# A Griffin-style encoder block: gates and branches by seven products, two of the weights' sums by accumulating DMAs

## The chip, the core and the metric

The kernel runs on one core of a Trainium2 chip. The engines of the core are named as the profile names them: PE (TensorE, matmuls), DVE (VectorE), ACT (ScalarE), POOL (GpSimd) and SP (SyncE, which here only issues DMAs). Each engine works through its own queue in order. The metric is the device time in microseconds of one execution; shorter is better. The kernel before takes 2479.7 us (median of 3 runs, 2479.21 to 2479.93).

## The reference

One layer over 512 tokens with 2048 features, all in float32:

```
h  = RMSNorm(x)
[q|k|v|u|ga|gb] = h @ W_in              # 3*1024 + 1024 + 2048 + 2048 columns
yA = attention(q, k, v)                 # 16 heads, 64-token chunks, 9-chunk band, relative bias
yB = pooling mixer(u)                   # trailing means over 2/4/8/16 tokens, per-group 256x256 map, scale
m  = sigmoid(ga) * (yA @ P_A) + sigmoid(gb) * (yB @ P_B)      # P_A, P_B: 1024 x 2048
x  = x + m @ W_o                        # 2048 x 2048
x  = x + (silu(g) * up) @ W_down        # [g|up] = RMSNorm(x) @ W_gate_up, 2048 x 11264; W_down 5632 x 2048
out = RMSNorm(x)
```

## The kernel before

**Precision.** Every float32 operand of a matmul is split into a rounded part (hi) and a rest (lo) in the float32r format, and every product is three matmuls into one PSUM bank: `product` (L210) and lines 925 to 927. A matmul has a 128x128 stationary operand and a 128x512 moving one. Weights arrive by SP's DMA queue in tiles of 128x1024 (512 KB); ACT copies such a tile to hi, DVE subtracts to get lo.

**First part, panels.** `panel` (L215) computes 256 output columns of h @ W for all 512 tokens, with the weights stationary and the turned x (XH, XL) moving. The order is q, k, v in four groups (with attention of the group's heads interleaved as generators), four panels of u (each followed by the generator `pooling`), and then the gates and branches: for yB the list `b_order` alternates panels of gate b and of P_B, for yA the list `a_order` does so with gate a and P_A. A gate panel is 16 x 2 x 3 = 96 matmuls and a branch panel 8 x 2 x 3 = 48; there are 8 of each for a and for b, so 16 x 96 + 16 x 48 = 2304 matmuls. The evacuations `evac_gate`, `evac_b` and `evac_a` multiply, add and store the merged m by features in DRAM (`m_dram`). At the end four P_A panels stand in a row (`N_TAIL`), and beside them `build_merged` builds the first forms for W_o.

**Second part, jobs.** `run_job` (L906) computes a block of 1024 inner rows by 1024 columns for all 512 tokens by a Strassen-like scheme with seven products P1, P5, P6, P3, P7, P2, P4 instead of eight block products; a product is 24 matmuls (two units of 12), a job 14 units and 168 matmuls where the direct way has 192. Here the activations are stationary, as seven prepared *forms* (`build_forms`, L721: for each of two halves seven hi by ACT, seven lo and four sums by DVE, each 128x512), and weights move. The seven weight operands come from four quarters of the weights, which are kept in tiles r11, r12, r21, r22 per unit: DVE adds r11 += r12 (for P5, L851), r11 += r22 (P6, L853), r12 += r22 (P7, L855) and r21 += r11 (P4, L857). `t_to`, `hi2_to` and `lo2_to` issue sum, hi and lo of a unit four, three and three units ahead of its matmuls, `load2_to` its load 7 units ahead.

The products of a job gather in PSUM in X (P1, P6, P7, P4) and Y (P5, P3; then a new Y for P2), and `evacuate` (L878) takes them out one unit after a product's end: as c tiles of a ring of six, which accumulate across products, and across jobs by accumulating DMAs of POOL's queue (`c += gp` and the like). What is done with a finished block is the job's `done`: storing partial results, squares, SiLU and product (`hidden`), turning by PE transposes (128x128) for the next forms. Such work is written as generators in the list `active`; `step()` runs each one's next stretch once per unit, so it fixes between which units of PE an instruction stands. There are 4 jobs for W_o (called o), 22 for W_gate_up (g; eleven for each half of the inner dimension), 12 for W_down (d; two with half the length): 36 x 168 + 2 x 84 = 6216 matmuls. Forms lie in two pools, A and B, used in turn.

**The end.** `last_done` and `store` (L1075, L1093) take the last d job's blocks through the final norm; `store(0)` for the first 256 tokens starts after block 11, `store(1)` after block 21.

Of the kernel before, what the change touches and what calls it, by code (L numbers as in the profile page):

```python
# [16 lines left out]
P = 128  # L17
# [15 lines left out]
PRODUCTS = ("P1", "P5", "P6", "P3", "P7", "P2", "P4")  # L33
# [13 lines left out]
def hybrid_block_kernel(  # L47
# [211 lines left out]
    for i in range(PWID // CU):  # L259
        add_panel(w_in, KD, 3 * AW + i * CU)  # L260
    GA, GB = 3 * AW + PWID, 3 * AW + PWID + D
    n_blk = D // CU
    b_order = [("g", 0), ("g", 1)] + [x for i in range(n_blk) for x in ((("y", i), ("g", i + 2)))]
    b_order = [x for x in b_order if x[1] < n_blk]
    for what, i in b_order:
        if what == "g":
            add_panel(w_in, KD, GB + i * CU)
        else:
            add_panel(w_branch_b, KB, i * CU)
    a_order = [x for i in range(n_blk - N_TAIL) for x in (("g", i), ("y", i))]  # L270
    a_order += [(what, i) for what in "gy" for i in range(n_blk - N_TAIL, n_blk)]
    for what, i in a_order:
        if what == "g":
            add_panel(w_in, KD, GA + i * CU)
        else:
            add_panel(w_branch_a, KA, i * CU)
# [100 lines left out]
    Q, K, KL, VS, YA = {}, {}, {}, {}, {}  # L377
    LOHALF, HIHALF = slice(0, DH), slice(DH, 2 * DH)
# [70 lines left out]
    def attention(h):  # L449
# [110 lines left out]
        nc.vector.tensor_tensor(YA[pair][hi_half], o_ps[LOHALF], low[LOHALF], op=ALU.add)  # L560

# [47 lines left out]
    YBH, YBL = {}, {}  # L609

    def pooling(g):
# [24 lines left out]
        for e in range(2):  # L636
# [6 lines left out]
            YBH[m], YBL[m] = split(ps, "yb", gains[:, 2 * KD + m:2 * KD + m + 1], mid)  # L643
            yield

    for i in range(PWID // CU):
        panel(KD, XH, XL, lambda oc, ps, i=i: evac_u(2 * i + oc, ps))
        active.append(pooling(i))


    SG, T = {}, {}
    m_dram = {}

    def evac_gate(m, ps):
        SG[m] = slot(F32, "sg")
        nc.vector.tensor_tensor(SG[m], ps, r_bc, op=ALU.mult)
        nc.scalar.activation(SG[m], SG[m], AF.Sigmoid)

    def evac_b(m, ps):
        T[m] = SG.pop(m)  # L660
        nc.vector.tensor_tensor(T[m], ps, T[m], op=ALU.mult)

    def evac_a(m, ps):
        s = SG.pop(m)
        nc.vector.tensor_tensor(s, ps, s, op=ALU.mult)
        nc.vector.tensor_tensor(s, T.pop(m), s, op=ALU.add)
        m_dram[m] = tc.dram_tile([P, 512], F32, name=f"m_dram{m}")
        nc.gpsimd.dma_start(m_dram[m], s)

    for what, i in b_order:  # L670
        if what == "g":
            panel(KD, XH, XL, lambda oc, ps, i=i: evac_gate(2 * i + oc, ps))
            if i == 1:
                drain()
        else:
            panel(KB, YBH, YBL, lambda oc, ps, i=i: evac_b(2 * i + oc, ps))
    YAH, YAL = {}, {}

# [547 lines left out]
```

## Time and profile before

| | |
|---|---|
| median of 3 runs | 2479.7 us |
| profiled execution: its own time / its span | 2477.76 us / 2476.0 us |
| PE busy / DVE busy / ACT busy / POOL busy | 2414.8 / 1734.9 / 1158.7 / 129.8 us |
| panels of q, k, v, u with attention | 0 to 422 us |
| gates and branches | 422 to 965 us |
| jobs o / g and d | 965 to 1129 us / 1129 to 2457 us |
| end (final norm, stores) | 2457 to 2476 us |
| moved by DMA | 352.19 MB, mean 142 GB/s |

The profile is of one execution. Its span runs from the first to the last instruction; the execution's own time is 1.8 us longer. PE is the engine that is busy nearly all of the time, so a microsecond in which PE has nothing to do is lost, and a matmul that falls away is gained, as long as nothing else takes its place. Stretches are given in us from the span's start.

### The profile page before, as it was taken

How to read it: one execution, taken by the hardware profiler on the slowest of the kernel's cores; microseconds unless marked ns; L12 is line 12 of the kernel's file. 1: busy time of each engine (PE TensorE's matmuls, PEld its weight loads, DVE VectorE, ACT ScalarE, POOL GpSimd, SP SyncE). 2: the span in 40 equal slices, each digit the busy share in tenths (PEclk: the TensorE clock that was granted, in tenths of full speed). 3: DMA queues.
4: the chain of work that ended last, by engine and by line, in shares of the span. 5: the costliest groups of instructions: out<-in, count | busy, mean ns of one | idle time of the engine just before them, and what ended most of it. 6: DMA issues, size and time to landing. Idle time of an engine off the chain costs nothing.

```text
span 2476.0 us, 28917 instructions
## 1 busy us (share of the span) xinstructions
PE 2414.8 (98%) x11221; PEld 2002.4 (81%) x11221; DVE 1734.9 (70%) x2026; ACT 1158.7 (47%) x1484; POOL 129.8 (5%) x226
## 2 busy tenths in 40 slices
PE   9999999999999999999999999989999999999996
PEld 7899888888888887787788888867788787887785
DVE  6556656523343338989787787888888888798977
ACT  5445443322222224467544544555645555555645
POOL 0000000000000001110000000001010000000010
PEclk9999999999999999999999999999999999999998
DMA  5322232233333335765354453657365555464564
GB/s 180 98 90 90 83 108 83 90 96 100 95 109 107 111 117 193 219 189 212 112 204 142 165 202 119 198 146 186 102 187 137 171 151 171 126 194 135 158 188 127
DMA packets 203145, 352.19 MB, mean 142 GB/s; under 512 B 11304, under 2 KB 95856, under 8 KB 202880
## 3 DMA queue, kind: packets, MB, share of 16 engines
q1 hardware_dynamic: 177616, 263.50, 31.0%
q0 software_dynamic: 24096, 84.49, 14.6%
q10 hardware_dynamic: 1296, 2.36, 0.2%
q8 instruction: 88, 1.44, 0.2%
q14 instruction: 49, 0.40, 0.0%
HBM read 289.44 MB, written 60.86 MB: 141 GB/s over the span
## 4 chain that ended last, share of the span: by engine, by line
PE 82%; DVE 11%; issue 3%; ACT 2%; DMA 0%; ACTq 0%; SPq 0%; DVEq 0%
PE psd L211 10%; PE psd L213 10%; PE psd L212 10%; PE psx L925 8%; PE psx L927 8%; PE psx L926 8%; PE psy L925 7%; PE psy L926 6%; PE psy L927 6%; DVE low L873 4%; DVE c L890 1%; ACT hiw L865 1%; PE psd L424 1%; PE psd L425 1%; PE psd L426 1%
## 5 line engine op out<-in xcount | busy, mean ns | idle before, releaser
L865 ACT ACTIVATE hiw<-r 128x1024 fp32r<-128x1024 f32 x518 | 546.8, 1059 | 556.6 <-PE psx L927 241.7
L873 DVE TENSOR_TENSOR low<-r,hiw 128x1024 fp32r<-128x1024 f32 x518 | 631.7, 1221 | 225.1 <-ACT hiw L865 224.5
L925 PE MATMUL psx<-low,fP 128*128 128x512 f32 x1184 | 467.0, 394 | 14.7 <-DVE c L890 7.3
L927 PE MATMUL psx<-hiw,fP 128*128 128x512 f32 x1184 | 462.3, 390 | 0.0
L926 PE MATMUL psx<-hiw,fP 128*128 128x512 f32 x1184 | 461.9, 390 | 0.0
L168 DVE TENSOR_TENSOR lo<-raw,hi 128x1024 fp32r<-128x1024 f32 (+1 forms) x161 | 195.8, 1218 | 309.4 <-ACT hi L159 309.2
L925 PE MATMUL psy<-low,fP 128*128 128x512 f32 x888 | 350.5, 395 | 23.3 <-DVE low L873 21.3
L159 ACT ACTIVATE hi<-raw 128x1024 fp32r<-128x1024 f32 (+1 forms) x161 | 169.2, 1053 | 416.5 <-PE psd L213 299.2
L927 PE MATMUL psy<-hiw,fP 128*128 128x512 f32 x888 | 346.1, 390 | 0.0
L926 PE MATMUL psy<-hiw,fP 128*128 128x512 f32 x888 | 345.8, 389 | 0.0
L211 PE MATMUL psd<-xh,lo 128*128 128x512 f32 x864 | 338.5, 392 | 0.0
L213 PE MATMUL psd<-xl,hi 128*128 128x512 f32 x864 | 336.8, 390 | 0.0
L212 PE MATMUL psd<-xh,hi 128*128 128x512 f32 x864 | 336.7, 390 | 0.0
L925 PEld LDWEIGHTS psx<-low,fP 128*128 128x128 f32 x1184 | 222.8, 188 | 67.9 <-DVE c L890 11.3
L927 PEld LDWEIGHTS psx<-hiw,fP 128*128 128x128 f32 x1184 | 222.8, 188 | 47.4
L926 PEld LDWEIGHTS psx<-hiw,fP 128*128 128x128 f32 x1184 | 223.0, 188 | 44.9
L925 PEld LDWEIGHTS psy<-low,fP 128*128 128x128 f32 x888 | 166.7, 188 | 65.6 <-DVE low L873 29.2
L927 PEld LDWEIGHTS psy<-hiw,fP 128*128 128x128 f32 x888 | 166.6, 188 | 35.5
L926 PEld LDWEIGHTS psy<-hiw,fP 128*128 128x128 f32 x888 | 166.8, 188 | 33.4
L213 PEld LDWEIGHTS psd<-xl,hi 128*128 128x128 f32 x864 | 162.2, 188 | 34.2
L212 PEld LDWEIGHTS psd<-xh,hi 128*128 128x128 f32 x864 | 162.4, 188 | 32.1
L211 PEld LDWEIGHTS psd<-xh,lo 128*128 128x128 f32 x864 | 162.3, 188 | 32.1
(205 smaller groups left out, 2789.5 us busy)
## 6 DMA issues: line engine op xcount, KB each, us to landing
r<-in_w_gate_up SPq DMA_DIRECT2D x176, 512.0 KB, 8.2
raw<-in_w_in SPq DMA_DIRECT2D x127, 512.0 KB, 3.6
r<-in_w_down SPq DMA_DIRECT2D x88, 512.0 KB, 7.7
x1d<-c POOLq DMA_DIRECT2D x48, 512.0 KB, 7.9
gp<-c POOLq DMA_DIRECT2D x44, 512.0 KB, 5.5
c<-gp POOLq DMA_DIRECT2D x33, 512.0 KB, 5.2
r<-in_w_out SPq DMA_DIRECT2D x32, 512.0 KB, 8.1
raw<-in_w_branch_b SPq DMA_DIRECT2D x16, 512.0 KB, 3.3
```

What stands on the lines that cost most here:

```text
L159: nc.scalar.activation(hi_t[i][:, :m], raw_t[i][:, :m], AF.Copy)
L168: nc.vector.tensor_tensor(lo_t[i][:, :m], raw_t[i][:, :m], hi_t[i].bitcast(F32)[:, :m], op=ALU.subtract)
L211: mm(ps, wl, ah, start=start, stop=False)
L212: mm(ps, wh, ah, start=False, stop=False)
L213: mm(ps, wh, al, start=False, stop=stop)
L424: mm(o, XH[kk][:, tok], hi[:, k], start=first, stop=False, skip_group_check=True)
L425: mm(o, XH[kk][:, tok], lo[:, k], start=False, stop=False, skip_group_check=True)
L865: nc.scalar.activation(hi_t[-1 - i], source(i), AF.Copy)
L873: nc.vector.tensor_tensor(lo_t[-1 - i], source(i), hi_t[-1 - i].bitcast(F32), op=ALU.subtract)
L925: mm(ps[:, t], fh, lo[:, k], start=first, stop=False, skip_group_check=True)
L926: mm(ps[:, t], fh, hi[:, k], start=False, stop=False, skip_group_check=True)
L927: mm(ps[:, t], fl, hi[:, k], start=False, stop=last, skip_group_check=True)
```

## The change

Gates and branches become jobs too. The jobs z (w_in's columns of gate b and gate a side by side, two inner halves, four column blocks), b and a (P_B and P_A, two column blocks each) come ahead of o, so there are 12 more jobs, 12 x 168 = 2016 matmuls in place of 2304. Their inputs are stored by features in DRAM and loaded for building: turned x (`xt_dram`), yA and yB (`y_dram`). Their outputs are by tokens: partial gates in `zp`, sigmoids in `sg`, gated yB in `td`; `gated` loads the sigmoid and multiplies, `a_done` then lets a DMA add `td` and turns the sum by PE transposes for the forms of o (`turned_all`, 64 transposes). Ahead of the first z job the last panel (u) is followed by `drain()`, in which pooling of the last panel and the forms of z from `xt_dram` are finished.

Products stand in the order P1, P5, P6, P2, P7, P3, P4; P2 has a bank pair of its own. `T_BY_DMA = ("P4", "P7")`: r12 += r22 and r21 += r11 are issued by POOL as accumulating DMAs from SBUF to SBUF; DVE keeps r11 += r12 and r11 += r22. A job waits (`while ... step()`) until its forms are written out in the program. The end stores the first 256 tokens after the last block's sums.

```diff
-PRODUCTS = ("P1", "P5", "P6", "P3", "P7", "P2", "P4")
+PRODUCTS = ("P1", "P5", "P6", "P2", "P7", "P3", "P4")
+A_WAIT = 2
-T_BY_DMA = False
+T_BY_DMA = ("P4", "P7")
...
+        nc.gpsimd.dma_start(xt_dram[k], xt)
...
+        if odd:
+            nc.gpsimd.dma_start(y_dram["a", pair], YA[pair])
...
-            YBH[m], YBL[m] = split(ps, "yb", gains[:, 2 * KD + m:2 * KD + m + 1], mid)
+            yb = slot(F32, "yb")
+            nc.scalar.activation(yb, ps, AF.Copy, scale=gains[:, 2 * KD + m:2 * KD + m + 1])
+            nc.gpsimd.dma_start(y_dram["b", m], yb)
...
             elif p == "P6":
                 nc.vector.tensor_tensor(run, run, r["22"], op=ALU.add)
-            elif p == "P7" and not T_BY_DMA:
-                nc.vector.tensor_tensor(r["12"], r["12"], r["22"], op=ALU.add)
-            elif p == "P4":
+                if "P7" in T_BY_DMA:
+                    nc.gpsimd.dma_start(r["12"], r["22"], accum_op=ALU.add)
+            elif p == "P7":
+                if "P7" not in T_BY_DMA:
+                    nc.vector.tensor_tensor(r["12"], r["12"], r["22"], op=ALU.add)
+                if "P4" in T_BY_DMA:
+                    lo2_to(j.at("P2", h) + 1)
+                    nc.gpsimd.dma_start(r["21"], run, accum_op=ALU.add)
+            elif p == "P4" and "P4" not in T_BY_DMA:
                 nc.vector.tensor_tensor(r["21"], r["21"], run, op=ALU.add)
...
-            if p in ("P5", "P2"):
+            if p == "P5":
                 Y = bank2("y")
-            ps = Y if p in ("P5", "P3", "P2") else X
+            ps = Y if p in ("P5", "P3") else bank2("x") if p == "P2" else X
...
+    def turned_all(forms, fb, cs, m0=None):
         half = yield from new_half()
         for n in range(4):
             ps = bank2("a")
             for tt in range(NT):
                 nc.tensor.transpose(ps[:, tt * P:(tt + 1) * P], cs[tt // 2][:, tt % 2, n * P:(n + 1) * P], ident)
             yield
...
+    def z_done(kb, p):
+        def gate(b, c):
+            th, f = int(b[0]) - 1, int(b[1]) - 1
+            for t in range(2):
+                nc.scalar.activation(c[:, t], c[:, t], AF.Sigmoid, scale=rstd[:, 2 * th + t:2 * th + t + 1])
+                yield
+            nc.gpsimd.dma_start(sg[f, p, th], c)
...
+    def gated(which, p, b, c):
+        s = ctile()
+        nc.sync.dma_start(s, sg[which, 2 * p + int(b[1]) - 1, int(b[0]) - 1])
+        yield
+        yield
+        nc.vector.tensor_tensor(c, c, s, op=ALU.mult)
...
+        def merge(b, c):
+            yield from gated(1, p, b, c)
+            nc.gpsimd.dma_start(c, td[p, b], accum_op=ALU.add)
+            ready[b] = c
+            if "1" + b[1] in ready and "2" + b[1] in ready:
+                fb = int(b[1]) - 1
+                for _ in range(A_WAIT):
+                    yield
+                yield from turned_all(get_forms(m_forms, p, "AB"[p], 2), fb, (ready["1" + b[1]], ready["2" + b[1]]))
...
+    order = [("z", kb, p) for kb in range(2) for p in range(4)]
+    order += [("b", 0, 0), ("b", 0, 1), ("a", 0, 0), ("a", 0, 1)]
+    order += [("o", kb, p) for kb in range(2) for p in range(2)] + [("g", 0, p) for p in range(NG)]
...
+    for n, i in enumerate(u_order):
...
+        panel(KD, XH, XL, lambda oc, ps, i=i: evac_u(2 * i + oc, ps))
+        active.append(pooling(i))
...
+    active.append(build_z0())
     spacing[0] = 0
     drain()
...
+        while key not in kept or kept[key]["built"] < j.nh:
+            step()
+        j.forms = kept[key]
         run_job(j)
+        left[j.forms["pool"]] -= 1
```

**Where the first forms are built, DVE.** Before, forms for the first job (fP5 and on, from s and half) stand between the weights' lo and the gating of the last P_A panels (sg):

```order
L736 TENSOR_TENSOR fP5_640_7283<-s_645_7345,fP5_640_7283 128x2x256
L747 TENSOR_TENSOR s_645_7345<-s_645_7345,half_643_7305 128x512
L168 TENSOR_TENSOR lo157_7395<-raw157_7255,hi157_7378 128x1024
L736 TENSOR_TENSOR fP7_640_7286<-s3_645_7346,fP7_640_7286 128x2x256
L738 SCALAR_TENSOR_TENSOR fP6_640_7284<-s_645_7345,fP6_640_7284 128x2x256
L749 TENSOR_TENSOR s_645_7345<-s_645_7345,half_643_7305 128x512
L168 TENSOR_TENSOR lo158_7430<-raw158_7312,hi158_7413 128x1024
L665 TENSOR_TENSOR sg_630_7001<-psd_646_7376,sg_630_7001 128x512
L666 TENSOR_TENSOR sg_630_7001<-sg_566_5343,sg_630_7001 128x512
L736 TENSOR_TENSOR fP2_640_7287<-half_643_7305,fP2_640_7287 128x2x256
L665 TENSOR_TENSOR sg_631_7016<-psd_647_7377,sg_631_7016 128x512
L666 TENSOR_TENSOR sg_631_7016<-sg_567_5358,sg_631_7016 128x512
```

Now they stand in a row behind the last u panel's evacuation (u), and the first sums of the weights for P5 (r11 and r12) and its lo (low2) come behind them:

```order
L593 TENSOR_TENSOR u_510_4411<-psd_475_4200,r_bc_153 128x512
...
L703 TENSOR_TENSOR s_524_4474<-half_516_4443 128x512
...
L699 TENSOR_TENSOR fP1_515_4436<-half_516_4443,fP1_515_4436 128x2x256
...
L240 TENSOR_TENSOR dl_529_4493<-d_527_4488,dh_528_4492 128x512
...
L699 TENSOR_TENSOR fP2_515_4439<-half_516_4443,fP2_515_4439 128x2x256
L699 TENSOR_TENSOR fP3_515_4441<-s_524_4474,fP3_515_4441 128x2x256
L699 TENSOR_TENSOR fP4_515_4442<-half_516_4443,fP4_515_4442 128x2x256
...
L699 TENSOR_TENSOR fP1_515_4436<-half_519_4455,fP1_515_4436 128x2x256
...
L699 TENSOR_TENSOR fP4_515_4442<-half_519_4455,fP4_515_4442 128x2x256
L806 TENSOR_TENSOR r11_472_4191<-r11_472_4191,r12_535_4565 128x1024
L806 TENSOR_TENSOR r11_473_4193<-r11_473_4193,r12_536_4567 128x1024
L834 TENSOR_TENSOR low2_4582<-r11_472_4191,hiw2_4580 128x1024
```

From the first to the last of these rows there are 40 rows on DVE: 4 of 128x1024, 30 of 128x512 and 6 small ones.

**Where o begins, PE.** Before, the last P_A panel's matmuls (psd) are followed by the first job's (psx), with nothing between:

```order
L211 MATMUL psd_654_7542<-yah_598_5900,lo160_7508 128x512
L212 MATMUL psd_654_7542<-yah_598_5900,hi160_7492 128x512
L213 MATMUL psd_654_7542<-yal_599_5901,hi160_7492 128x512
L925 MATMUL psx_659_7637<-low0_7539,fP1_640_7282 128x512
L926 MATMUL psx_659_7637<-hiw0_7537,fP1_640_7282 128x512
```

Now the first o job (fP1 of 747) follows the last a job (fP4 of 672) with 20 transposes of the a jobs' sums between them, each row here two transposes; c_762 is the last block of the a job (its P4):

```order
L885 MATMUL psx_730_7749<-hiw167_8041,fP4_672_6889 128x512
L886 MATMUL psx_730_7749<-hiw167_8041,fP4_672_6889 128x512
L933 MATMUL psa_765_8123<-ident_105,c_746_7921 128x128 x2
...
L933 MATMUL psa_766_8134<-ident_105,c_746_7921 128x128 x2
...
L933 MATMUL psa_767_8142<-ident_105,c_746_7921 128x128 x2
...
L933 MATMUL psa_768_8150<-ident_105,c_746_7921 128x128 x2
...
L933 MATMUL psa_772_8170<-ident_105,c_735_7812 128x128 x2
L933 MATMUL psa_772_8170<-ident_105,c_762_8109 128x128 x2
L884 MATMUL psx_773_8175<-low168_8063,fP1_747_7924 128x512
```

The DMA that adds td to c_762 stands on POOL, and the multiplication ahead of it on DVE, between the a job's end and these rows.

**The sums of a g job, DVE and POOL.** Before, on DVE, r12 += r22 and r21 += r11 stand between the lo of the units:

```order
L873 TENSOR_TENSOR low174_11198<-r22_867_11063,hiw174_11196 128x1024
L855 TENSOR_TENSOR r12_864_11022<-r12_864_11022,r22_867_11063 128x1024
L873 TENSOR_TENSOR low175_11217<-r22_868_11081,hiw175_11215 128x1024
L855 TENSOR_TENSOR r12_866_11042<-r12_866_11042,r22_868_11081 128x1024
L873 TENSOR_TENSOR low176_11234<-r12_864_11022,hiw176_11232 128x1024
L873 TENSOR_TENSOR low177_11254<-r12_866_11042,hiw177_11252 128x1024
...
L857 TENSOR_TENSOR r21_873_11176<-r21_873_11176,r11_862_10984 128x1024
L873 TENSOR_TENSOR low179_11293<-r21_874_11194,hiw179_11291 128x1024
L857 TENSOR_TENSOR r21_874_11194<-r21_874_11194,r11_863_11002 128x1024
L873 TENSOR_TENSOR low180_11313<-r21_873_11176,hiw180_11311 128x1024
L890 TENSOR_TENSOR c_875_11212<-c_875_11212,psx_869_11118 128x1024
```

Now these four stand on POOL, between the accumulating DMAs that add gp to the c tiles:

```order
L810 DMA r12_1083_13257<-r22_1088_13298 128x1024
L810 DMA r12_1086_13278<-r22_1089_13318 128x1024
L847 DMA c_1097_13433<-gp2_11_3397 128x1024
L847 DMA c_1098_13473<-gp2_22_3400 128x1024
L816 DMA r21_1090_13338<-r11_1078_13214 128x1024
L816 DMA r21_1092_13360<-r11_1081_13236 128x1024
L847 DMA c_1100_13516<-gp2_12_3398 128x1024
```

On DVE the rows of lo follow each other there without them.

## Rows read from the trace of the kernel before

**Rows 1.** The page: busy time of the engines, and slices of the span.
```profile
PE 2414.8 (98%) x11221; PEld 2002.4 (81%) x11221; DVE 1734.9 (70%) x2026; ACT 1158.7 (47%) x1484; POOL 129.8 (5%) x226
...
PE   9999999999999999999999999989999999999996
...
DVE  6556656523343338989787787888888888798977
...
PEclk9999999999999999999999999999999999999998
DMA  5322232233333335765354453657365555464564
```

**Rows 2.** Windows: stretch, length, busy by engine (instructions), clock, DMA share, GB/s.
```profile
422.00:965.00 543.00, 543.00 (x2400) 449.85 (x2399) 209.97 (x252) 142.43 (x165) 8.18 (x15) 1.00 0.33 104
965.00:1129.00 164.00, 158.65 (x709) 129.02 (x708) 145.81 (x146) 94.56 (x122) 21.26 (x28) 1.00 0.73 222
1129.00:1555.00 426.00, 422.60 (x1874) 348.54 (x1873) 342.81 (x311) 220.78 (x236) 23.70 (x45) 1.00 0.46 165
1555.00:2457.00 902.00, 872.68 (x3877) 711.59 (x3875) 768.57 (x742) 493.81 (x580) 69.52 (x81) 1.00 0.55 156
1300.00:1340.00 40.00, 40.00 (x178) 33.14 (x177) 29.96 (x27) 20.01 (x20) 2.14 (x4) 1.00 0.44 158
2010.00:2091.00 81.00, 79.92 (x359) 65.62 (x358) 73.82 (x77) 47.16 (x57) 6.45 (x8) 1.00 0.64 182
1672.00:1676.00 4.00, 4.00 (x19) 3.10 (x17) 2.74 (x3) 2.35 (x3) 0.00 (x0) 1.00 1.06 200
5.00:12.00 7.00, 4.25 (x18) 3.23 (x17) 3.54 (x5) 4.57 (x8) 0.98 (x3) 0.76 0.99 335
```

**Rows 3.** Waits of PE: line waited for, us in total, times, longest.
```profile
PE psy L925 <- DVE low L873: 21.3, 21, 2.2
PE psx L925 <- DVE c L890: 7.3, 10, 1.6
PE psx L925 <- ACT c L884: 5.0, 1, 5.0
...
PE psx L925 <- DVE low L873: 2.3, 5, 0.6
```

**Rows 4.** Groups by line: operation, shapes, count, busy us, mean ns of one.
```profile
L873 DVE TENSOR_TENSOR low<-r,hiw 128x1024 fp32r<-128x1024 f32 x518 | 631.7, 1221 | 225.1 <-ACT hiw L865 224.5
...
L857 DVE TENSOR_TENSOR r<-r,r 128x1024 f32<-128x1024 f32 x74 | 90.3, 1220 | 1.0
...
L855 DVE TENSOR_TENSOR r<-r,r 128x1024 f32<-128x1024 f32 x74 | 90.1, 1218 | 0.0
L884 ACT ACTIVATE c<-psx 128x1024 f32<-128x1024 f32 x76 | 76.7, 1009 | 0.0
...
L736 DVE TENSOR_TENSOR fP<-half,fP 128x512 fp32r<-128x512 f32 x57 | 38.9, 683 | 0.0
...
L624 DVE COPY s<-s 128x2 f32<-128x2 f32 (+2 forms) x12 | 1.9, 162 | 0.0
```

**Rows 5.** Timeline of PE around the longest wait: start, us, operation [wait before it].
```profile
1642.88 0.39 PE L927 MATMUL psy<-hiw,fP 128*128 128x512 f32 x1
1648.25 0.80 PE L925 MATMUL psx<-low,fP 128*128 128x512 f32 x1 [4.99 <-ACT c L884]
...
1653.11 0.58 PE L927 MATMUL psx<-hiw,fP 128*128 128x512 f32 x1
1653.53 0.60 PE L953 MATMUL psa<-ident,c 128*128 128x128 f32 x4
1653.89 0.48 PE L925 MATMUL psy<-low,fP 128*128 128x512 f32 x1
```

**Rows 6.** DMA issues: queue, count, KB each, median us from issue to landing.
```profile
c<-gp POOLq DMA_DIRECT2D x33, 512.0 KB, 5.2
```

**Rows 7.** The line L886 alone, accumulating DMAs into c: their landing.
```profile
DMA to landing us min/median/max: 5.1/5.2/10.0
```

**Rows 8.** Timeline of the end: last matmul, last block's sum, last stores.
```profile
2456.79 0.39 PE L927 MATMUL psx<-hiw,fP 128*128 128x512 f32 x1
...
2459.38 1.28 DVE L896 TENSOR_TENSOR c<-c,psx 128x512 f32<-128x512 f32 x2
...
2470.68 0.72 ACT L1111 ACTIVATE c<-c,fin 128x512 f32<-128x512 f32 x1 [0.41 <-ACT c L1111]
2471.43 0.34 ACTq L1112 DMA_DIRECT2D out<-c  x1
```

More of the change, by code (lines that the diff above doesn't have):

```diff
@@ L258, in hybrid_block_kernel @@
             add_panel(w_in, KD, part * AW + i * CU, cuts=FIRST_CUTS if i == part == 0 else None)
[L259 removed]
+    u_order = list(reversed(range(PWID // CU)))
+    for i in u_order:
         add_panel(w_in, KD, 3 * AW + i * CU)
     GA, GB = 3 * AW + PWID, 3 * AW + PWID + D
[L262 to L276, printed above, removed]
     x_cols = [(0, 128), (128, 128), (256, 256), (512, 512), (1024, 512), (1536, 512)]
@@ L696, in forms_pool, with get_forms @@
             tc.tile_pool(name=f"forms{which}", bufs=1, side=side, reuse_waits="tile"))
+    left = {"A": 0, "B": 0}
+    def get_forms(kept, key, which, n):
+        while key not in kept and left[which]:
+            yield
+        if key not in kept:
+            left[which] = n
+            kept[key] = new_forms(which)
+            kept[key].update(pool=which, built=0)
+        return kept[key]
     def new_forms(which):
@@ L751, in build_forms, with build_from @@
         low(*plan[-1])
-    def build_merged(forms, kb):
+    def build_from(forms, tiles):
         hs = []
@@ L974, in x1_turned @@
             yield
-            m = KD + p * 8 + fb * 4 + n
-            nc.scalar.activation(half[:, n // 2, n % 2], ps, AF.Copy, scale=gains[:, m:m + 1])
-        if p not in gu_forms:
-            gu_forms[p] = new_forms("AB"[p])
-        yield from build(gu_forms[p], fb, half)
+            g = 1.0 if m0 is None else gains[:, m0 + n:m0 + n + 1]
+            nc.scalar.activation(half[:, n // 2, n % 2], ps, AF.Copy, scale=g)
+        f = yield from forms
+        yield from build(f, fb, half)
     def wait_then(n, g):
@@ L1052, in build_down @@
         last = b == n_down - 1
-        while gates_run[0] < NG if last else down_run[0] < 2 * b:
-            yield
-        if b not in d_forms:
-            d_forms[b] = new_forms("B" if last else "A")
-        yield from build(d_forms[b], h, hid.pop(p))
+        f = yield from get_forms(d_forms, b, "B" if last else "A", 2)
+        yield from build(f, h, hid.pop(p))
     n_down = (NG + 1) // 2
@@ L1086, in rest, with end, rows_then, rows @@
                     nc.vector.tensor_tensor(y[:, t], y[:, t], gf[:, f0:f0 + 512], op=ALU.mult)
+                if p == 0 or blk == "22":
                     yield
-        if p == 1 and blk in ("11", "21"):
-            active.append(in_turn(rest(), store(th)))
-        else:
-            active.append(wait_then(3 if blk == "12" else 0, rest()))
-    def store(th):
-        r = fin[:, 0, 2 * th:2 * th + 2]
-        ss = ssq2[:, 2 * th:2 * th + 2]
-        row_rstd(ss, r, r3[:, 0, 2 * th:2 * th + 2], r3[:, 1, 2 * th:2 * th + 2])
+        def end():
+            store(0, "v")
+            rows(1)
+            store(0, "s")
+            store(1, "vs")
+            yield
+        if (p, blk) == (1, "12"):
+            active.append(in_turn(rest(), rows_then(0)))
+        elif (p, blk) == FINAL:
+            active.append(in_turn(rest(), end()))
+        else:
+            active.append(rest())
+    def rows_then(th):
+        rows(th)
         yield
+    def rows(th):
+        k = slice(2 * th, 2 * th + 2)
+        row_rstd(ssq2[:, k], fin[:, 0, k], r3[:, 0, k], r3[:, 1, k])
+    def store(th, engines):
         for t in range(2):
@@ L1165, in hybrid_block_kernel, with build_y, build_z1 @@
     ps2 = late.enter_context(tc.tile_pool(name="psum2", bufs=1, space=bass.MemoryType.PSUM, reuse_waits="tile"))
-    o_forms = {0: fo}
-    def build_o1():
-        o_forms[1] = new_forms("B")
-        yield from build_merged(o_forms[1], 1)
+    y_forms = {}
+    def build_y(which):
+        f = yield from get_forms(y_forms, which, "B" if which == "a" else "A", 2)
+        yield from build_from(f, [y_dram[which, j] for j in range(KA)])
+    def build_z1():
+        f = yield from get_forms(z_forms, 1, "B", 4)
+        yield from build_from(f, xt_dram[8:])
     load2_to(LOAD_AHEAD - 2)
```

185 lines of the change are left out of this document (85 added, 100 removed).

## The prediction

> **What bounds the kernel now.** I read the page first. PE is busy 98% of the span, in nines from the first slice to the last but one, at full clock [rows 1]; so the question is which matmuls go and which idle time comes. Next came windows by stage: gates and branches (422 to 965 us) have PE busy all of 543.00 us, with DVE at 209.97 us and a DMA share of 0.33 [rows 2]. That stage is bound by the number of matmuls alone: 543.00 us / 2400 = 0.2263 us each. In the jobs PE idles 5.35 + 3.40 + 29.32 = 38.1 us (o, first g half, the rest), and DVE fills 89%, 80% and 85% of these stretches. The waits say for whom PE idles: 21.3 + 7.3 + 2.3 = 30.9 us for DVE, 5.0 us once for ACT [rows 3]. So the jobs sit just under a second limit, DVE.
>
> **The change part by part.** The sum is made against the profiled execution, 2477.8 us; the median of the runs stands 1.9 us above it.
>
> Matmuls: 288 go, 288 x 0.2263 = -65.2 us.
>
> Transposes for the forms of o: 64, in 16 fours. A four took 0.36 us from its start to the next matmul's, and 0.60 us to its own end [rows 5]: 16 x 0.36 to 0.60 = +5.8 to +9.6; I take +8. (The features-by-token form before needed none.)
>
> u to z: here the panels end and the first forms have no cover. On DVE 40 rows stand from the last u evacuation to the lo of P5: 4 of 1.22 us, 30 of 0.68 us, 6 of 0.16 us [rows 4] = 26.3 us. Some waits for the loads of the halves fall inside; I count none. Until then PE has the 24 pooling matmuls of the last two groups and P1's 24, 48 x 0.2263 = 10.9 us. PE loses 15.4 us. After such a pause the clock comes back at half: behind the wait of 4.99 us twelve matmuls ran some 0.43 us apart instead of 0.23 [rows 5], about 2.4 us lost; I take 3. The z1 forms (two halves of 11 rows of 0.68 us, 15 us of DVE) in the first z job add 3 more, since DVE starts it with no lead. Together +21.5; from below 11 (DVE gets half its rows done before PE ends, as pooling of earlier groups may), from above 32 (the loads of both halves fall inside, 5 us each).
>
> Builds in z, b and a beside other jobs: DVE has per job 14 lo and 4 sums of 1.22, 3 or 4 evacuations of 1.22, with gating 4 products more, 31 us, and with a build 46 us against 38.0 us of PE; the lead of two units (5 us) and the next, lighter job take most. I take +5.5 for the three such jobs and for the first transposes inside the second a job, where PE may wait for a DMA; bounds 0 and 15.
>
> a to o: PE's queue has 20 transposes ahead of the first o matmul, and the last two need block 21 of the last a job. After the last matmul (E) that block goes through ACT's copy (1.01 us), DVE's product, POOL's accumulating DMA (5.2 us from issue [rows 6]). On DVE, between P3's evacuation and that product, stand 12 rows: 4 of 1.22 and 8 of 0.68, 10.3 us. P3 ends two units (5.4 us) before E, so the product is done at about E - 5.4 + 1.2 + 10.3 + 1.2 = E + 7.3 and the DMA at E + 13 with some time for POOL. Of these 13 us 2.5 are transposes already counted, so 10.5 us idle, and 2.5 us for the clock: +13. Bounds: 6 (DVE idle in time: 1.01 + 1.22 + 5.2 less the transposes, without clock) and 20.
>
> TensorE's clock in that stretch: from 5 to 12 us of the span PE mostly transposes x between waits, and the granted clock was 0.76 in the mean [rows 2], that is part of it at 1.2 instead of 2.4 GHz. The Trainium skill says in "TensorE: Matmul & The Clock Gate", Part 4: PE-mode transpose, that transposes do not count as PE's work for the clock the way matmuls do; by it the whole stretch between a and o would count as idle and the 2.5 us be sure, and without it they would shrink toward none.
>
> Two sums off DVE: 4 rows per job, 4 x 1.22 = 4.9 us of 38. In the jobs there before that is 90.1 + 90.3 = 180 us of DVE [rows 4]. It is worth only what PE waits for DVE, 30.9 us; the waits at P5 and P6 keep their sums, the evacuation of P3 no longer stands before P2. I take 60%: -19; bounds 0 and -31. Where this relief fails, DVE is as full as before and nothing is lost.
>
> The same sums as DMAs: issued when the unit four ahead is prepared, needed as source of hi five units later, 5 x 12 x 0.2263 = 13.6 us. An accumulating DMA of this size from DRAM took 5.2 us in the median and 10.0 us at most [rows 6, 7]; none within SBUF is in the trace. So each hides, unless POOL issues it late. What they take from the DMA engines: in a stretch of accumulating DMAs the share stood at 1.06, which I read as full, and 200 GB/s were moved [rows 2]: 0.524 MB / 200 GB/s = 2.6 us of all engines, four per job 10.5 us. Busy before, per job: o 0.73 / 1.06 x 41 = 28.2 us, second g half (0.64) 24.5, first g half (0.44) 15.8. With the sums 38.7, 35.0 and 26.3 us against 38.0 us. z of the second half moves as much as o, and a nearly so; ten jobs stand at the limit. For late landings there I take +8; bounds 0 and +55 (below).
>
> The DMA stalls by a rule: The Trainium skill, "DMA: Bandwidth & Descriptors", SWDGE vs HWDGE vs iDMA, says that each DMA engine serves the queue that POOL fills and the one that SP fills in turn. By it a sum that meets a burst of weight loads goes at about half its rate. The longest accumulating DMA, 10.0 us against the median of 5.2 [rows 7], fits that; the third rival is what it would do here.
>
> P2 in its own bank: takes away the wait of P2 for P3's evacuation (part of the 30.9) and costs no instruction; X of the next job takes P2's bank, free for six units, so no new wait.
>
> End: before, from the last matmul's end (2457.2) to ACT's last store 14.6 us, with six scaled copies and stores of the second half on ACT at 1.14 us [rows 8]. Now four of those, and two of the first half, stand behind the second sqrt, but DVE takes six of the first half's tiles: last store near E + 12; -2.5, bounds -4 and +3.
>
> Sum: -65.2 + 8 + 21.5 + 5.5 + 13 - 19 + 8 - 2.5 = -30.7. 2477.8 - 30.7 = 2447; on the median of runs 2449.
>
> **The rivals.**
>
> First, the pauses close: DVE has the early rows of the build done, the c tiles come in time, the relief is full. For it speaks that 30.9 of 38.1 us of PE's idle time is DVE's; against it the two places in the order where nothing else is there for PE. -65.2 + 8 + 11 + 0 + 6 - 31 + 0 - 2.5 = -73.7: 2406.
>
> Second, slower: the sums inside SBUF fill the DMA engines. Read and written on the same memory, a sum could cost more than the 2.6 us of one from DRAM. The place is every job with much other traffic, and the point from which it decides is where four sums fill the rest of a job: (38.0 - 28.2) / 4 = 2.5 us in o, 3.4 in the second g half, 5.6 in the first. At 4 us: 6.2 us late in each of ten jobs (z1, a, o) and about 1 us in each of 21 g and d jobs, 62 + 21 = 83 in place of the 8: 2449 + 75 = 2524. Nearer the point (3.3 us) it would be 3.4 x 10 = 34: 2475, which is no loss. For it: the share of 0.73 in o, and rows 1, where slices already have 7. Against it: the first g half has room, and gates before o ran at 0.33.
>
> Third, the sums are not too dear but late: POOL's queue is in order, and a sum stands behind accumulating DMAs that wait for evacuations. A wait of two units (5.4 us) and 10.0 us of landing are 15.4 us against 13.6: 1.8 us of PE. In one of the two pairs of a third of the 50 jobs that is 30 us: 2479, no change. POOL's waits for evacuations are long in total, but they are where it had nothing else to do, so they do not tell.
>
> That the change does not do what it says is ruled out by the order: the transposes, the matmuls and the DMAs stand there.
>
> **How the numbers follow.** About what a run of this kernel can tell from no change is 0.2%, 5 us: 2474.7 to 2484.7. The forecast gets 0.55 (its own range 2430 to 2468, all faster), the first rival 0.17, the second 0.14, the third 0.14. Faster: 0.55 + 0.17 + 0.03 of the third = 0.75. Same: 0.08 of the third. Slower: 0.14 + 0.03 = 0.17. For the range I leave out the far halves of the first and the second rival, about 0.17 in all: 2415 to 2488.
>
> **What would show it.** Right: PE's count falls by about 224 (288 matmuls less 64 transposes); two gaps of PE, 12 to 20 us behind the last u panel and 8 to 13 us before o, both with the granted clock at 1.2 GHz at their end; PE's waits for DVE in the old jobs at a third of 30.9 us; sums landing in 5 to 8 us, and hardly any wait of ACT for them. Wrong: ACT's hi waiting for r12 or r21 in most jobs (third rival); DMA shares at 1.0 through whole z1, a and o jobs with PE waiting for weights (second); no gap at a to o, or PE's waits in the g jobs as before, which would make the forecast wrong in either direction.

## The result, and the profile after

The changed kernel takes 2445.4 us (median of 4 runs, 2444.29 to 2447.09) against 2479.5 us before on the same chip: ratio 0.9865, 95% interval 0.9851 to 0.9879. The profiled execution took 2447.1 us with a span of 2445.3 us, 30.7 us less than before; the forecast's sum was -30.7. That the total fits so well is partly luck: the profiled execution is the slowest of the four, by the medians 34.1 us are gained (2445.4 where the forecast had 2449), and the terms fit less well than their sum.

The page of the kernel after, for [rows 1]: busy time, and the span in 40 slices.

```profile
PE 2369.2 (97%) x10997; PEld 1968.5 (81%) x10997; DVE 1765.2 (72%) x2049; ACT 1310.1 (54%) x1661; POOL 349.6 (14%) x498
...
PE   8999999899999997999999999999999999999996
...
DVE  5556566886867868868766666677868778687966
...
PEclk9999999899999998999999999999999999999998
DMA  6333333777999887996777777879798798798795
```

PE has 224 instructions less, as forecast. Its first slice is an 8 now and its sixteenth (a to o) a 7; the clock dips in the sixteenth and in the eighth (u to z). Windows of the kernel after, for [rows 2]: second half of z; the a jobs; o; first half of g; the rest.

```profile
618.00:774.00 156.00, 153.51 (x671) 125.07 (x671) 115.86 (x109) 95.72 (x113) 32.74 (x43) 1.00 0.98 274
...
860.00:965.00 105.00, 88.10 (x398) 72.29 (x397) 77.07 (x79) 54.03 (x68) 16.64 (x20) 0.90 0.86 221
965.00:1125.00 160.00, 154.38 (x702) 127.51 (x701) 124.19 (x125) 98.15 (x135) 34.55 (x43) 0.99 0.94 260
1125.00:1547.00 422.00, 422.00 (x1864) 349.30 (x1863) 289.34 (x260) 214.17 (x220) 60.99 (x86) 1.00 0.74 216
1547.00:2428.00 881.00, 867.28 (x3874) 714.87 (x3872) 671.00 (x654) 495.16 (x581) 146.40 (x169) 0.99 0.83 210
```

DVE's share in the jobs fell (0.69 and 0.76 of the last two stretches, 0.80 and 0.85 before), the DMA share rose to 0.74 to 0.98. PE's waits of the kernel after, for [rows 3]:

```profile
PE psa L933 <- DMA c<-t: 16.8, 2, 13.6
PE psy L884 <- DVE low L834: 12.9, 10, 5.2
PE psa L933 <- ACT half L936: 5.6, 3, 4.8
PE psx L884 <- DVE c L851: 5.2, 2, 4.0
PE psa L211 <- ACT dh L239: 4.4, 2, 2.3
...
PE psx L884 <- DVE low L834: 1.7, 2, 0.8
```

Waits for DVE fell from 30.9 us in 36 stops to 19.8 us in 14; in o, g and d alone they are 9.8 us, the third that the prediction named as its sign. The longest wait is new: transposes (L933) that wait for the DMA that adds td.

For the rest of the text I use one number per stage: its *extra time*, that is from the first matmul of its jobs to the first of the next stage, less 0.2273 us for each of its matmuls (the full-clock distance in the trace). Idle time, half-clock time and transposes are in it. Worked out from the profiled executions:

| us | z | b | a (2nd) | o | g | d | first z matmul at |
|---|---|---|---|---|---|---|---|
| before | | | | 11.5 | 28.4 | 39.4 | |
| after | 11.4 | 3.6 | 27.7 | 14.6 | 12.9 | 29.9 | 457.5 |

**a to o.** PE, DVE and POOL of the kernel after: the last matmul of the second a job, the transposes, the first of o; the last two gating products; the DMAs behind them.

```profile
939.97 0.39 PE L886 MATMUL psx<-hiw,fP 128*128 128x512 f32 x1
953.94 4.50 PE L933 MATMUL psa<-ident,c 128*128 128x128 f32 x20 [13.58 <-DMA c<-t]
958.20 0.47 PE L884 MATMUL psx<-low,fP 128*128 128x512 f32 x1
```
```profile
945.82 1.22 DVE L993 TENSOR_TENSOR c<-c,c 128x1024 f32<-128x1024 f32 x1
...
948.28 0.68 DVE L699 TENSOR_TENSOR fP<-s,fP 128x512 fp32r<-128x512 f32 x1
948.88 1.22 DVE L993 TENSOR_TENSOR c<-c,c 128x1024 f32<-128x1024 f32 x1
```
```profile
947.60 0.89 POOL L1009 DMA_DIRECT2D c<-t  x1 [5.16 <-issue]
950.80 0.87 POOL L1009 DMA_DIRECT2D c<-t  x1 [2.31 <-DVE fP L701]
```

The chain is the predicted one, with DVE's products behind the forms' rows. But the first 16 transposes need the first of these two DMAs, that of P3's block, issued 7.6 us after the last matmul; PE's stop ended with it, one DMA earlier than the one that I had followed. From 943.7 to 957.3 us the granted clock was 0.50.

**u to z.** On DVE the last u evacuation starts at 444.32, and the first lo of P5 ends at 468.96: 24.6 us, where I had 26.3.

```profile
444.32 0.69 DVE L593 TENSOR_TENSOR u<-psd,r_bc 128x512 f32<-128x512 f32 x1 [0.71 <-PE psd L213]
```
```profile
467.73 1.23 DVE L834 TENSOR_TENSOR low<-r,hiw 128x1024 fp32r<-128x1024 f32 x1
```

**The sums as DMAs and the end.** The 196 sums within SBUF land in 6.1 us in the median (the DMA list after; [rows 6] for one from DRAM), and ACT waited 5.5 us in all for them, most of it in one stop in the second d job:

```profile
r<-r POOLq DMA_DIRECT2D x196, 512.0 KB, 6.1
```
```profile
1668.88 2.95 ACT L826 ACTIVATE hiw<-r 128x1024 fp32r<-128x1024 f32 x3 [4.38 <-DMA r<-r]
```

From the last matmul (2427.92) to the last store's issue (2440.64) the end took 12.7 us, against 14.6 in [rows 8].

```profile
2427.92 0.39 PE L886 MATMUL psx<-hiw,fP 128*128 128x512 f32 x1
```
```profile
2440.64 0.34 ACTq L1138 DMA_DIRECT2D out<-c  x1
```

### The profile page after: what moved, and what is told of

It reads as the page before. It is cut to its first block, busy times and chain, and to the rows that moved or that the text cites. A ratio compares the mean times of both kernels' runs of the same rounds, so it can differ in the third digit from the quotient of the medians.

```text
span 2445.3 us, 29833 instructions
## 1 busy us (share of the span) xinstructions
PE 2369.2 (97%) x10997; PEld 1968.5 (81%) x10997; DVE 1765.2 (72%) x2049; ACT 1310.1 (54%) x1661; POOL 349.6 (14%) x498
## 3 DMA queue, kind: packets, MB, share of 16 engines
q1 hardware_dynamic: 158656, 278.97, 32.6%
## 5 line engine op out<-in xcount | busy, mean ns | idle before, releaser
L834 DVE TENSOR_TENSOR low<-r,hiw 128x1024 fp32r<-128x1024 f32 x686 | 837.9, 1223 | 476.7 <-ACT hiw L826 475.6
L826 ACT ACTIVATE hiw<-r 128x1024 fp32r<-128x1024 f32 x686 | 725.8, 1060 | 730.8 <-PE psx L886 449.5
L884 PE MATMUL psx<-low,fP 128*128 128x512 f32 x1960 | 770.6, 393 | 10.8 <-DVE c L851 5.2
L886 PE MATMUL psx<-hiw,fP 128*128 128x512 f32 x1960 | 765.3, 390 | 0.0
L885 PE MATMUL psx<-hiw,fP 128*128 128x512 f32 x1960 | 765.1, 390 | 0.0
L884 PEld LDWEIGHTS psx<-low,fP 128*128 128x128 f32 x1960 | 369.8, 189 | 90.1 <-DVE c L851 6.0
L886 PEld LDWEIGHTS psx<-hiw,fP 128*128 128x128 f32 x1960 | 369.2, 188 | 77.6
L885 PEld LDWEIGHTS psx<-hiw,fP 128*128 128x128 f32 x1960 | 369.7, 189 | 75.4
L884 PE MATMUL psy<-low,fP 128*128 128x512 f32 x784 | 310.4, 396 | 12.9 <-DVE low L834 12.9
L886 PE MATMUL psy<-hiw,fP 128*128 128x512 f32 x784 | 307.3, 392 | 0.0
L886 PEld LDWEIGHTS psy<-hiw,fP 128*128 128x128 f32 x784 | 148.5, 189 | 31.5
L211 PE MATMUL psd<-xh,lo 128*128 128x512 f32 x352 | 139.7, 397 | 0.0
L213 PE MATMUL psd<-xl,hi 128*128 128x512 f32 x352 | 137.5, 391 | 0.0
L212 PE MATMUL psd<-xh,hi 128*128 128x512 f32 x352 | 137.4, 390 | 0.0
L816 POOL DMA_DIRECT2D r<-r x98 | 89.5, 914 | 323.2 <-DVE low L834 319.8
L810 POOL DMA_DIRECT2D r<-r x98 | 89.4, 992 | 281.8 <-DVE r L806 241.4
L851 DVE TENSOR_TENSOR c<-c,psx 128x1024 f32<-128x1024 f32 x100 | 121.4, 1214 | 0.0
```

The lines of the kernel that those rows point to most:

```text
L211: mm(ps, wl, ah, start=start, stop=False)
L212: mm(ps, wh, ah, start=False, stop=False)
L213: mm(ps, wh, al, start=False, stop=stop)
L810: nc.gpsimd.dma_start(r["12"], r["22"], accum_op=ALU.add)
L816: nc.gpsimd.dma_start(r["21"], run, accum_op=ALU.add)
L826: nc.scalar.activation(hi_t[-1 - i], source(i), AF.Copy)
```

## The experiments

All were timed against the kernel before, whose median was 2479.5 to 2479.7 each time; in brackets the 95% interval of the ratio to it. Differences between experiments are taken against 2445.4 us of the kernel after.

### Which sum is it worth to take from DVE

```diff
-T_BY_DMA = ("P4", "P7")
+T_BY_DMA = ()          # e1_sums_on_dve
+T_BY_DMA = ("P7",)     # e4_p7_by_dma
+T_BY_DMA = ("P4",)     # e9_p4_by_dma
```

> The kernel after with both sums (r12 += r22 and r21 += r11) back on DVE; order, banks and jobs as after. Theory: the relief in the o, g and d jobs (24.7 us less idle PE than before) comes from DVE's sums that fell away, 4 x 1.22 us per job in 50 jobs; then they come back as waits for DVE at the lo of P5 and P6 and at sums: 2445 + 25 = 2470 us (2462 to 2485), DVE busy up by about 200 us, PE's waits for DVE at 30 us or more. Rival: the relief is from P2's place and its own bank; then 2445 to 2451 us, and PE's waits for DVE stay near 20 us.

> The kernel after with the sum for P7 alone by DMA; the sum for P4 (r21 += r11) back on DVE, 2 x 1.22 us per job. Theory (DVE's load sets the relief): between the kernel after and the one with both sums on DVE, nearer to after since half the load is gone: 2445 + 8 = 2453 us (2447 to 2462). Rival (sums by DMA cost as much in late landings as they free): 2440 to 2446 us, no loss from taking one of the two DMAs away.

> The kernel after with the sum for P4 alone by DMA; the sum for P7 on DVE as before, 2 x 1.22 us per job. Theory: what counts is where in the job DVE is full, from P7's evacuation to the next job's sum for P5; the sum of P4 stood there, that of P7 stood where DVE waits for ACT anyway (e4_p7_by_dma freed 107 us of DVE and gained nothing). So 2445 to 2449 us. Rival: the two sums have to go together, since DVE's load as a whole must fall under a limit: 2458 to 2470 us.

Measured: 2476.8 us with none by DMA (0.9977 to 0.9995), 2480.1 with P7's (0.9994 to 1.0012), 2444.2 with P4's (0.9840 to 0.9867). So e1's theory holds, with 31.4 us, and e4 broke it in its first form (neither its theory nor its rival had the time): half of DVE's relief bought nothing, 3.3 us were even lost. e9 settled it: P4's sum alone gives all of it, 32.6 us against e1. The line of lo on DVE, in e1, e4, e9 and after (busy and mean, then idle time and its cause), says where freed time went:

```profile
L834 DVE TENSOR_TENSOR low<-r,hiw 128x1024 fp32r<-128x1024 f32 x686 | 837.0, 1222 | 290.9 <-ACT hiw L826 286.2
```
```profile
L834 DVE TENSOR_TENSOR low<-r,hiw 128x1024 fp32r<-128x1024 f32 x686 | 837.5, 1222 | 401.4 <-ACT hiw L826 400.0
```
```profile
L834 DVE TENSOR_TENSOR low<-r,hiw 128x1024 fp32r<-128x1024 f32 x686 | 837.9, 1223 | 365.4 <-ACT hiw L826 364.0
```
```profile
L834 DVE TENSOR_TENSOR low<-r,hiw 128x1024 fp32r<-128x1024 f32 x686 | 837.9, 1223 | 476.7 <-ACT hiw L826 475.6
```

Taking P7's 98 sums (120 us) off DVE made it wait 114 us longer for ACT: they had filled a hole. P4's 98 sums became 78 us of waiting. Their place, in a g job of e1 and then of e9 (DVE, [idle before]):

```profile
1247.08 1.22 DVE L851 TENSOR_TENSOR c<-c,psx 128x1024 f32<-128x1024 f32 x1
1248.21 1.22 DVE L818 TENSOR_TENSOR r<-r,r 128x1024 f32<-128x1024 f32 x1
1249.35 1.22 DVE L834 TENSOR_TENSOR low<-r,hiw 128x1024 fp32r<-128x1024 f32 x1
1250.48 1.22 DVE L818 TENSOR_TENSOR r<-r,r 128x1024 f32<-128x1024 f32 x1
1251.62 1.22 DVE L834 TENSOR_TENSOR low<-r,hiw 128x1024 fp32r<-128x1024 f32 x1
1252.75 1.22 DVE L851 TENSOR_TENSOR c<-c,psx 128x1024 f32<-128x1024 f32 x1
```
```profile
1228.09 1.21 DVE L851 TENSOR_TENSOR c<-c,psx 128x1024 f32<-128x1024 f32 x1
1229.62 1.23 DVE L834 TENSOR_TENSOR low<-r,hiw 128x1024 fp32r<-128x1024 f32 x1 [0.32 <-ACT hiw L826]
1232.34 1.23 DVE L834 TENSOR_TENSOR low<-r,hiw 128x1024 fp32r<-128x1024 f32 x1 [1.49 <-ACT hiw L826]
1233.48 1.22 DVE L851 TENSOR_TENSOR c<-c,psx 128x1024 f32<-128x1024 f32 x1
```

P4's sums (L818) stand between two evacuations (L851), ahead of the one of P7 for which P4's matmuls wait; the stretch has no idle time. This job itself loses nothing (from the third job on, the first half of g has no extra time in any of these kernels); where more rows come to it, the evacuation can be late. PE waits 16 times for an evacuation on that line in e1 and in e4 (12.2 and 10.6 us), twice in the kernel after, both times in the two short d jobs. Against the kernel after, e1 has 16.4 us more extra time in o, g and d, and 14.9 in z, b and a.

### The order of the products

```diff
-PRODUCTS = ("P1", "P5", "P6", "P2", "P7", "P3", "P4")
+PRODUCTS = ("P1", "P5", "P6", "P3", "P7", "P2", "P4")   # and P2 in a new Y; P7 alone by DMA
```

> The kernel after with the products in the order of before (P1, P5, P6, P3, P7, P2, P4) and P2 in a new Y as before; the sum for P7 by DMA and that for P4 on DVE, so it is to be compared with e4_p7_by_dma (2480 us), which differs in order and bank alone. Theory: P2's place and bank took away waits of PE for DVE's evacuations (some 5 us of the o, g and d jobs, and as much again in z, b and a); 2488 us (2484 to 2500). Rival: order and bank are worth nothing by themselves, they only make room for the sum of P4 to be issued two products early; 2478 to 2482 us.

Measured: 2499.6 us (1.0062 to 1.0087), 19.5 more than e4. P2's place and bank are worth that by themselves, with P4's sum on DVE: extra time in o, g and d is 92.2 us against 74.9 of e4. It is also 13 us above the 79.3 of the kernel before, which has these products too; 5 us of that are from o to g and 8 in the last two d jobs, where PE waits for DVE. Why it waits there and not before is not shown.

### a to o

```diff
-                for _ in range(A_WAIT):
+                for _ in range(A_WAIT if p == 0 else 8):              # e2_late_turn_a
-    order += [("b", 0, 0), ("b", 0, 1), ("a", 0, 0), ("a", 0, 1)]
+    order += [("b", 0, 0), ("a", 0, 0), ("b", 0, 1), ("a", 0, 1)]     # e10, e11
-N_C = 6
+N_C = 7                                                              # e11, with A_WAIT = 5
```

> The kernel after, where the second inner half's transposes of the merged sums (a_done, p = 1) wait 8 units in place of 2, so none stands ahead of the first o matmul and they go between the units of the first o job. Theory: PE lost the time at a to o because its queue held 20 transposes there that waited for the accumulating DMA of the last block (13.6 us, and the half clock behind it); 2445 - 14 = 2431 us (2427 to 2436). Rival: DVE is late there anyway with the builds of the first inner half's forms, and PE waits for these instead: 2441 to 2444 us, with new waits of 8 us or more for DVE in the first o job.

> The kernel after with the jobs b and a in the order b0, a0, b1, a1 (before: b0, b1, a0, a1). The transposes of the first a job then go into b1 and the builds of the first o forms stand at the start of a1 and no longer in its second half; the second a job's transposes go between the units of the first o job. Theory: a to o is slow because DVE has the builds of the first o forms and the gating products in one job, with PE's transposes stuck behind the last of them; with 38 us more lead the stretch closes: of about 28 us there 18 to 24 come back, 2425 us (2420 to 2430). Rival: the DVE rows only move and stall b1 and a1 as much: 2440 to 2448 us.

> As e10_a_between_b, and the transposes of an a job's sums wait 5 units in place of 2 (with a seventh c tile, for whose space the scratch of the squares is kept in 8 bits; nothing reads it). Theory: in e10 the gain at a to o was given back because PE met the transposes 2 units after the sums' DMA was issued and stood still until it landed (7.0 and 3.9 us, the longest wait in the first o job); with 5 units (13.6 us) the DMA has landed: the extra time of b, a and the first o job falls from 32 to about 12 us, 2428 us (2422 to 2434). Rival: DVE is the limit there (it is 98% full in the second a job of e10), and the time is 2442 to 2449 us with waits for DVE in place of those for the DMA.

e2: 2445.4 us (0.9851 to 0.9878), no gain: the rival's mechanism, though it asked for 2441 to 2444 us and a wait of 8 us. PE no longer waits 13.6 us for the DMA, but 4.8 us for another one and 5.1 us for the forms of o, and extra time only moves, from 27.7 (a) and 1.4 us (first two o jobs) to 10.8 and 17.1:

```profile
PE psa L933 <- DMA c<-t: 5.2, 2, 4.8
PE psx L886 <- DVE fP L699: 5.1, 1, 5.1
```

e10: 2448.6 us (0.9860 to 0.9890), just above the rival's range: the second a job's extra time fell to 1.6 us, as expected. But the first a job got 7.6, where PE waits for lo (4.6 us; the rival had such waits in the two jobs behind it), and the second b job 7.8 and the first two o jobs 15.3, where the transposes met DMAs that had not landed. e11 gave them time: 2437.5 us (0.9816 to 0.9843), 8 us better than after; I had 17, and the time lies between its theory and its rival. PE's waits from 770 to 1010 us, e10 and then e11:

```profile
PE psa L933 <- DMA c<-t: 10.7, 3, 7.0
PE psy L884 <- DVE low L834: 6.7, 3, 4.6
```
```profile
PE psy L884 <- DVE low L834: 7.0, 4, 4.6
PE psx L884 <- DVE low L834: 2.1, 3, 0.8
```

Extra time of b, a and the first two o jobs: 32.6 us after, 32.3 in e10, 21.9 in e11, where the waits for the DMA are gone and those for DVE stay. So both causes stood in line, the transposes' place on PE's queue and DVE's rows; taking one away showed the other.

### The first panel

```diff
+                xt_late.append((k, xt))   # e3: all 16 stores written behind the first q panel
+            nc.gpsimd.tensor_copy(after_x, XL[k].bitcast(F32)[:, :1])   # e3b: and POOL waits for the last x
```

> The kernel after, where the 16 stores of turned x to DRAM (256 KB each, POOL's queue) are issued behind the first q panel and not one by one in it. Theory: the first q panel ends 6.8 us later than before because these stores share the DMA engines with the first loads of x and of weights; 2445 - 6 = 2439 us (2437 to 2441), and the first panel ends near 61 us. Rival: the loss there is ACT's or PE's own work (the second copy of x, the order of turning): 2444 to 2446 us, and the first panel ends near 68 us.

> As e3_late_xt, but with a small POOL copy that reads the last turned x tile ahead of the 16 stores, so that they are really held back until x is turned (in e3 POOL's queue ran ahead and issued them nearly as in the kernel after). Theory: the stores share the DMA engines with the first loads; the first q panel then ends near 39 us (38.5 before, 42.6 to 45.3 in kernels with the stores) and the time is 2440 us (2438 to 2443). Rival: something else at the start costs these 4 to 7 us: panel end at 42 us or later, 2445 to 2447 us.

(61 and 68 us in e3's text are the end of the second panel; the first ended at 38.5 before and 45.3 after.) e3: 2446.6 us (0.9852 to 0.9879). It did not test its theory: POOL's queue had nothing ahead of the stores, so they left as early as before (the first at 6.52 us, at 6.99 in the kernel after). e3b did: first panel's end at 40.4 us, 2442.6 us (0.9835 to 0.9862). Its interval overlaps that of the kernel after, so the time alone doesn't prove the gain; the panel's end speaks for it, since eleven profiled kernels with early stores have it between 41.9 and 46.7, and e8, the other one with late stores, at 39.6. The first 30 us, before, after and e3b:

```profile
0.00:30.00 30.00, 26.05 (x132) 20.22 (x133) 18.28 (x41) 21.19 (x36) 3.76 (x12) 0.94 0.75 257
```
```profile
0.00:30.00 30.00, 22.36 (x99) 16.55 (x100) 13.22 (x31) 19.14 (x31) 9.73 (x23) 0.87 0.90 317
```
```profile
0.00:30.00 30.00, 25.36 (x119) 19.54 (x120) 16.07 (x37) 21.80 (x35) 3.75 (x12) 0.89 0.72 248
```

### u to z

```diff
-    u_order = list(reversed(range(PWID // CU)))
+    u_order = list(range(PWID // CU))
```

> The kernel after with the four u panels in the other order, so that the pooling group with the longest window (four steps of sums in place of one) is the last ahead of the first z job. Between the last u evacuation and P5's first lo DVE then has 15 rows more (six sums and two closing rows of 0.68 us, the rest small): about 6.7 us. Theory: u to z is bound by DVE's chain of rows, so the time there grows by these rows, 5 to 8 us: 2452 us (2449 to 2455), with the wait for P5's lo or the pooling parts longer by as much. Rival: the stretch waits for the loads of the halves or for ACT, and the rows fit into DVE's idle time: 2444 to 2447 us.

Measured: 2470.9 us (0.9948 to 0.9975), 25.5 more than after: the right direction, and far too small a size. DVE's rows grew by 7 us as worked out, but r12 had not landed when they ended, and DVE stood still:

```profile
476.19 0.69 DVE L699 TENSOR_TENSOR fP<-half,fP 128x512 fp32r<-128x512 f32 x1 [0.40 <-ACT fP L706]
482.10 2.50 DVE L806 TENSOR_TENSOR r<-r,r 128x1024 f32<-128x1024 f32 x2 [5.22 <-DMA r<-in_w_in]
```

The pooling's own matmuls waited 15.8 us for dh (4.4 us in the kernel after), and the last u evacuation started 4.4 us later. The load is late because SP's queue stood at it until a store of yB, the result of pooling, had landed; the loads there began at 478.31 us, and at 446.77 in the kernel after:

```profile
SPq L788 <- DMA yb_dram<-yb: 27.7, 1, 27.7
```

### More traffic

```diff
                 nc.vector.tensor_tensor(run, run, r["22"], op=ALU.add)
+                for _ in range(2):
+                    nc.gpsimd.dma_start(extra[n_extra[0] % 16], r["22"])
```

> The kernel after with two more DMAs of 512 KB per pair of weight units, stores of r22 from SBUF to a scratch in DRAM that nothing reads, in POOL's queue ahead of the sum for P7: about 100 MB more, as many DMAs as the two sums are. It shows how far the DMA engines and POOL's queue are from the point where late sums or late weights cost time. Theory (from the kernel after, where shares of 0.9 to 0.98 in z, a and o cost nothing): room for little in these ten jobs but for much in g and d: 10 to 40 us, all of it in z (second half), a and o. Rival: the share is no measure of room, since engines that move short pieces count as busy: 0 to 5 us. Other rival: sums come late everywhere, as predicted for the case where they fill the engines: 60 us or more, with ACT waiting for r12 and r21.

Measured: 2469.9 us (0.9947 to 0.9973), 24.5 more: the theory's size, but mostly at other places. The window of the second half of z, ACT's wait for sums, and the longest wait of DVE at the start of b:

```profile
618.00:774.00 156.00, 153.50 (x672) 125.08 (x671) 114.94 (x108) 95.20 (x112) 41.42 (x59) 1.00 1.05 317
```
```profile
ACT hiw L831 <- DMA r<-r: 44.6, 21, 5.2
```
```profile
DVE s L703 <- DMA half<-ya_dram: 8.7, 1, 8.7
```

Extra time grew by 11.0 us in b, 4.9 in the second a job, 4.3 in o, 4.8 in d, and by nothing in the second half of z, where the share rose to 1.05. So the share doesn't say where it hurts; late landings do. In o and d they are sums: ACT waited 18.4 us for them in o and 21.3 in the later g and d jobs. In b it is a half of yA for the next forms, which SP loads. The profile of e2, which has no added traffic, has the same stop with 5.6 us and 7.3 us more extra time in b than the kernel after, so not all of the 11.0 need come from the traffic. Accumulating loads of x1p landed in 14.2 us instead of 7.0, weights for g in 5.7 instead of 5.2, the halves of yA in 16.0 instead of 11.7. POOL's queue, which had the added work, slowed most, SP's less. The Trainium skill says in "DMA: Bandwidth & Descriptors", SWDGE vs HWDGE vs iDMA, that an engine takes its internal queues in turn; that the weights for g nearly keep their rate agrees, the halves of yA don't show it.

### All together

```diff
+T_BY_DMA = ("P4",)   # with e3b, e11, and wait_then(2 if p == 0 else 6, ...) in o_done
```

> What the runs point to, together: the sum for P4 alone by DMA (e9), the stores of turned x held back (e3b), b and a in turn with 5 units of wait and seven c tiles (e11), and the second inner half's transposes of the o jobs 6 units later in place of 2. Theory: each acts at its own place, so they add: 2444 - 3 - 17 - 4 = 2420 us (2414 to 2428). Rival: what is gained at a to o and o to g turns into waits for DVE's builds: 2436 to 2442 us.

Measured: 2428.1 us (0.9781 to 0.9807), at the upper edge of the theory's range and 17 us under the kernel after. Extra time from o to g (the last two o jobs and the first half of g) is 13.8 us, 14.9 after: there the later transposes moved the wait into g and bought 1 us.

## Why the prediction was right, and where it was not

- **Matmuls:** -65.2, measured -65 (8232 matmuls in jobs, 6216 + 2304 before).
- **u to z:** +21.5, measured about 17: 9 us of gaps and half clock ahead of z, and 7.6 us in its first half. The chain of DVE rows was sized right (24.6 of 26.3 us), and it set the time: DVE was busy in 24.3 of the 24.9 us from 444.3 on. I put PE's idle time too high, 15.4 us; it was 10.1 in four stops, since the matmuls there, in part at half clock, took 14.8 us and not 10.9. So the gap of 12 to 20 us that I named as a sign did not come. e12 agrees that the rows set it, and shows the loads that I left out, which wait for pooling.
- **Builds, and transposes with a to o:** +5.5 and +8 +13, measured 7.4 (second half of z 3.8, b 3.6) and 27.7. The mechanism stood as put, but for the block whose DMA ended the stop; the wait was 13.6 us where I had 10.5, and the first a job's transposes waited for their DMA as well (3.2 us, and a stretch at half clock), which I had only as a possibility.
- **Relief of DVE:** -19, measured -24.8 in the first two o jobs, the second half of g and d, or about -28.7 without the late sum of the next point. The step's reason was half wrong: I counted four rows per job off DVE, and two of them (P7's) are worth nothing. P4's place among the evacuations and P2's order and bank carry it. From o to g (the last two o jobs, the first half of g) 2.9 us were lost that I had not named, which leaves about -25.8.
- **DMA sums:** +8, measured about 3.9, all in the second d job. It has half the length, so P4's sum is needed three units after its issue and not five: 3 x 12 x 0.2273 = 8.2 us, where I had 13.6 for all jobs. The sum landed in 9.0 us (6.4 in e9), ACT waited 4.4 us for it (1.7 in e9), and PE 4.0 us for the evacuation behind it. The job's extra time is 5.6 to 8.7 us in the eight profiled kernels with both sums by DMA, 1.5 to 2.8 in the five with one or none. So a sum came late in one job of 50, as the third rival has it, but through the short cover and not behind DMAs that wait for evacuations. Where four sums would fill the rest of a job, the second rival's point, is not shown; e7, with twice the sums' DMAs, cost 24.5 us.
- **Start:** 0, measured +6.8 in this execution. I cost the 16 stores of turned x at nothing without naming their cover; the first loads already had the DMA engines 75% busy. With the stores held back 1.9 of the 6.8 us stay in e3b, whose cause is open.
- **End:** -2.5, measured -1.9 to the last store's issue.

The sum of what was measured is -65 + 6.8 + 17 + 7.4 + 27.7 - 25.8 + 3.9 - 1.9 = -29.9 of -30.7. The forecast's total rests on errors that cancel: start, a to o and builds were 15 us too low, u to z, the sums and the relief 15 us too high. The first rival failed since both gaps are there. Of the second nothing showed, of the third one late sum, with another cause.

## What to carry to other kernels

Ask of a row taken off a busy engine whether it stood in a stretch without idle time or in a hole: here 120 us off DVE were worth nothing at one place and 33 us at another. When an instruction that waits for a DMA is put into a queue in order, count the whole chain to the landing, in the shortest job too, and look at what is late behind it before moving it. A store added to a stretch that loads can have a price, even on an idle queue, and in e3 writing it later in the program didn't delay it, since its queue had nothing to wait for.

## What was not expected of the hardware

512 KB sums from SBUF into SBUF landed in 6.1 us in the median beside other traffic at shares of 0.74 to 0.98, and PE lost time to them in one job only. At a to o the 20 transposes, after 13.6 us of idle time, took 4.50 us at half clock; in e11, where they stand between matmuls, the granted clock was 1.00 from 940 to 990 us. The Trainium skill says in "TensorE: Matmul & The Clock Gate", Part 4: PE-mode transpose, that transposes don't count for the clock as matmuls do; the idle time ahead of them hides here what they would do alone, so no run tells.
